# Tiles of the split products moved to one address modulo 512 bytes, and half-height products padded with zero rows, in a two-layer RWKV / Conformer trunk

## The chip, the cores and the metric

One core of a Trainium2 chip runs one program. The metric is the device time of one execution in microseconds (us); a profiled execution shows every instruction of the five engines: TensorE (PE, its weight loads apart as PEld), VectorE (DVE), ScalarE (ACT), GpSimd (POOL) and SyncE (SP), which issues the DMAs. Lower is better.

## The reference, cut to what matters

```
for layer in range(2):                        # x: 512 tokens x 1024 features, float32
    h = rmsnorm(x, g_mix[layer])
    x = x + (rwkv7_time_mix(h) if layer == 0 else conformer_conv(h))
    x = x + memory_cross_attention(rmsnorm(x, g_x[layer]), memn, ...)
    x = x + conv_ffn(rmsnorm(x, g_f[layer]), ...)      # 1024 -> 2 x 2816 -> 1024
return rmsnorm(x, g_final)
# inside the time mix, H = 16 heads of 64 features:
logw  = -softplus(-(w0 + tanh(xw @ w1) @ w2)) - 0.5    # w1: 1024 x 64, w2: 64 x 1024
a     = sigmoid(a0 + (xa @ a1) @ a2)                   # a1: 1024 x 64, a2: 64 x 1024
g     = sigmoid(xg @ g1) @ g2                          # g1: 1024 x 160, g2: 160 x 1024
y     = groupnorm_per_head(recurrence(r, decay, k, v, kk, a))
out   = ((y + sum(r * k * r_k, per head) * v) * g) @ w_o
```

## The kernel before

Features lie on the 128 partitions, the 512 tokens along each partition. The recurrence is computed in chunks of 64 tokens. The order of work is that of the code, with a scheduler's priorities deciding where the streams of two parts meet on an engine.

Every large product is a **split product**. A float32 operand is cast to the type float32r by ACT (its high part) and DVE subtracts the high part from the original (its low part), in `split` (L176, L177); a product is then three float32r matmuls, in `mm3`: high x high (L181), high x low (L182), low x high (L183). The first operand of a matmul is the stationary one (loaded into the array by a weight load of 128 columns, 512 bytes of a partition), the second the moving one (512 columns, 2048 bytes of a partition). In the profile a group is written out<-moving,stationary: `g<-xh,wl` is moving tile xh against weights wl. `wsplit` fetches 512 KB of weights into a `raw` tile and splits it into `wh` and `wl`, two buffers of each. The moving tiles differ by stage: `xh`, `xl` (the normed input of the r, k, v, query, Conformer-in and FFN-in products), `BK` (into w_o), `oh`, `ol` (into the attention's output), `ah`, `al` (into the FFN's second product) and `vh`, `vl` (into the Conformer's second product).

Three small products of the time mix use fewer than 128 rows of the array. In `k_done`, for each of the 8 pairs of heads p, w2 and a2 are each used as a full product with `zw` or `za` (L507: 128 rows, both halves of z, once with the high and once with the low part of w2) and one of 64 rows with `zl` (L508). In `rowbcast` (L475, called twice for each p in `rwkv_out`) a row of 0 and 1 in `selb` spreads a row of per-head numbers over 64 partitions, with 64 rows of the array. In `rwkv_out` the last 32 rows of g2 are a product of 96 rows (L815).

Tiles are placed by pools that stand one behind the other; in a pool the tiles stand one behind the other too, each rounded up to 32 bytes. Where a tile begins follows from all that stand ahead of it. In the built program the operands of the split products begin, modulo 512 bytes, at:

| operands (moving against stationary) | moving | stationary | difference |
|---|---|---|---|
| xh, xl against wh, wl | 32 | 160 | 128 |
| ah, al against wh, wl (FFN, second product) | 160 | 160 | 0 |
| oh, ol against wh, wl (attention output) | 160 | 160 | 0 |
| km against qh, ql (attention scores) | 160 | 160 | 0 |
| vh, vl against wh, wl (Conformer, second product) | 384 | 160 | 288 |
| BK against wh, wl (time mix, w_o) | 256 | 160 | 416 |
| ph, pl against vm (attention values) | 288 | 160 | 384 |

A slice of weights is 512 bytes long and a moving tile 2048, so the difference is the same for all products of a row. Some products are plain float32: `raw` against `kvm` (L931) begins at 160 against 160 in 24 of its products and at 160 against 256 in 8.

Of the kernel before, what the change touches and what calls it, by code (L numbers as in the profile page):

```python
# [8 lines left out]
F32 = mybir.dt.float32  # L9
F32R = mybir.dt.float32r  # L10
# [7 lines left out]
KT = D // 128  # L18
# [8 lines left out]
CW = 31  # L27
KAPPA = float(np.exp(-0.5))
NTMP = 6
# [81 lines left out]
class Builder:  # L111
# [212 lines left out]
    def rwkv(self):  # L324
        nc, a = self.nc, self.a
        with ExitStack() as cx:
            r1 = self.pool(cx, "r1")
# [11 lines left out]
            units = self.key_units(0, mem) + self.value_units(0, mem)  # L339
            for j in range(NU0):  # L340
                units.pop(0)(lambda: t4[:, j % 2, :])
            cpr = self.t(r1, [128, 11 * KT], "cpr")
            hw0, ha0, hka, cka, nkk = (cpr[:, j * KT : (j + 1) * KT] for j in range(5))
            self.cc = (hw0, ha0, hka, cka, nkk)
            vv = lambda n, w=1: self.vecs[:, VEC[n] : VEC[n] + w * KT]
# [8 lines left out]
            h = self.x  # L354
# [5 lines left out]
            rs = self.rstd_tail([acc], 0)  # L360
# [14 lines left out]
            ps = self.ps()  # L375
            for i in range(KT):
                for m, w, o in ((1, w1, 0), (4, a1, 64)):
                    nc.tensor.matmul(ps[o : o + 64, :], w[:, i * 64 : (i + 1) * 64], mix(m, i, "xh", KT),
                                     start=i == 0, stop=i == KT - 1)
# [91 lines left out]

    def rowbcast(self, half, p):
        ps = self.ps("h")
        rows = slice(64 * half, 64 * half + 64)
        self.nc.tensor.matmul(ps, self.selb[rows, p * 128 : (p + 1) * 128], self.rows[rows], start=True, stop=True)  # L475
        return ps

    def k_done(self, p, psk):

        nc, a = self.nc, self.a  # L480
        hw0, ha0, hka, cka, nkk = self.cc
        vv = self.vec
        k, ec = self.AR[:, 0, p, :], self.AR[:, 1, p, :]
        as3 = lambda x_: x_.rearrange("p (c t) -> p c t", t=C)
        nc.scalar.copy(k, psk)
        sq = self.tmp()
        nc.scalar.activation(sq, psk, AF.Square, scale=vv("kk", p))
        pq = self.ps("h")
        for c2 in range(4):
            nc.tensor.matmul(pq[:, 2 * c2 : 2 * c2 + 2], sq[:, c2 * 128 : (c2 + 1) * 128], self.c("head"),  # L490
                             start=True, stop=True)
        rho = self.rho[:, p * NCH : (p + 1) * NCH].rearrange("p (a b) -> p a b", b=2)
        for h in range(2):
            for e in range(2):
                nc.vector.tensor_scalar_max(rho[64 * h : 64 * h + 64, :, e],
                                            pq[64 * e : 64 * e + 64, 0:8].rearrange("p (a b) -> p a b", b=2)[:, :, h], 1e-24)
        nc.vector.reciprocal(self.rho[:, p * NCH : (p + 1) * NCH], self.rho[:, p * NCH : (p + 1) * NCH])
        w2 = self.t(self.r1, [128, 2, 128], "w2", bufs=W2B)
        nc.sync.dma_start(w2, a["wa2"][p])
        ws = self.t(self.gp, [128, 2, 128], "tmp", F32R, bufs=NTMP)  # L500
        nc.scalar.copy(ws, w2)
        pl = []
        for h, z in enumerate((self.zw, self.za)):
            own, oth = slice(64 * h, 64 * h + 64), slice(64 - 64 * h, 128 - 64 * h)
            nc.vector.tensor_tensor(out=ws[oth, h], in0=w2[oth, h], in1=ws[oth, h], op=ALU.subtract)
            ps = self.ps("h")
            nc.tensor.matmul(ps, ws[:, h], z, start=True, stop=False)  # L507
            nc.tensor.matmul(ps, ws[own, h], self.zl[own], start=False, stop=True)  # L508
            pl.append(ps)
        pw, pa = pl  # L510
        th = self.tmp()
        nc.scalar.activation(th, pw, AF.Tanh, bias=hw0[:, p : p + 1], scale=0.5)
        half = self.eps[:, 3:4]
        nc.scalar.activation(th, th, AF.Identity, bias=half, scale=0.5)
        cum = self.tmp()
        nc.vector.tensor_tensor_scan(out=cum, data0=self.c("scan"), data1=th, initial=0.0, op0=ALU.mult, op1=ALU.add)
        nc.scalar.activation(ec, cum, AF.Exp, scale=-KAPPA)
        emc = self.tmp()
        nc.scalar.activation(emc, cum, AF.Exp, scale=KAPPA)
        nc.vector.tensor_copy(self.G[:, p * 8 : p * 8 + 8].unsqueeze(2), as3(ec)[:, :, C - 1 : C])  # L520
        ta = self.tmp()
        nc.scalar.activation(ta, pa, AF.Tanh, bias=ha0[:, p : p + 1], scale=0.5)
        km = self.tmp()
        nc.scalar.activation(km, ta, AF.Identity, bias=cka[:, p : p + 1], scale=hka[:, p : p + 1])
        nc.scalar.activation(ta, ta, AF.Identity, bias=half, scale=0.5)
        BK = self.t(self.r1, [128, NCH, 2, C], "BK", bufs=NP)
        self.bk[p] = BK
        nc.vector.tensor_tensor(out=ta, in0=ta, in1=emc, op=ALU.mult)
        kp = km
        nc.vector.tensor_tensor(out=kp, in0=k, in1=km, op=ALU.mult)  # L530
        for h in range(2):
            rows = slice(64 * h, 64 * h + 64)
            nc.vector.scalar_tensor_tensor(out=BK[rows, :, h, :], in0=as3(k)[rows], scalar=vv("kk", p)[rows],
                                           in1=as3(ta)[rows], op0=ALU.mult, op1=ALU.mult)
            nc.vector.tensor_tensor(out=BK[rows, :, 1 - h, :], in0=as3(kp)[rows], in1=as3(emc)[rows], op=ALU.mult)
        k3, e3 = as3(k), as3(ec)
        nc.vector.scalar_tensor_tensor(out=k3[:, :, 1:], in0=k3[:, :, 1:], scalar=nkk[:, p : p + 1],
                                       in1=e3[:, :, : C - 1], op0=ALU.mult, op1=ALU.mult)
        nc.vector.tensor_scalar_mul(k3[:, :, 0:1], k3[:, :, 0:1], nkk[:, p : p + 1])
# [220 lines left out]
    def rstd_rows(self, tt):  # L760
# [4 lines left out]
        for q in range(2):  # L765
# [6 lines left out]
            for j in range(4):  # L772
                p = q * 4 + j
                nc.tensor.matmul(var[:, 2 * p : 2 * p + 2], sq[:, j, :], self.c("head"), start=True, stop=True)
        rs = self.t(self.gp, [128, 32], "rst", bufs=1)
        nc.vector.memset(rs, 1.0)
        nc.scalar.activation(rs[:, 0:16], var[:, 0:16], AF.Sqrt, bias=self.eps[:, 1:2], scale=1.0 / HD)
        nc.vector.reciprocal(rs[:, 0:16], rs[:, 0:16])
# [7 lines left out]
    def rwkv_out(self):  # L786
        nc, a = self.nc, self.a
        AR, V = self.AR, self.V
        slot = lambda dt=F32: self.t(self.r1, [128, 1024], "c4", dt, bufs=4)
        late, selb = slot(), slot(F32R)  # L790
        nc.sync.dma_start(late, a["late"][:, 0:1024])
        self.selb = selb
        nc.scalar.copy(selb, late)
        g1, g2 = self.gates
        zg1 = self.xtile()
        self.split(g1, *zg1)
        zg2 = self.t(self.gp, [128, T], "xh", F32R, bufs=KT)
        nc.scalar.copy(zg2[0:96], g2[0:96])
        nc.vector.tensor_tensor(out=zg2[32:64], in0=g2[32:64], in1=zg2[32:64], op=ALU.subtract)
        self.filler(FP)  # L800
        outs = []
        for p in range(NP):
# [9 lines left out]
                nc.vector.tensor_tensor(out=lo, in0=raw[64:96, :, 128:256], in1=lo, op=ALU.subtract)  # L812
            pgt = self.ps()
            self.mm3(pgt, gh[:, p % 2, 0:128], gl[:, p % 2, :], *zg1, True, False)
            nc.tensor.matmul(pgt, gh[0:96, p % 2, 128:256], zg2[0:96], start=False, stop=True)  # L815
            pr = self.rowbcast(1, p)
            yn = self.tmp()
            nc.vector.tensor_tensor(out=yn, in0=y, in1=pr, op=ALU.mult)
# [121 lines left out]
    def xattn(self, layer):  # L940
        nc, a = self.nc, self.a
        kd, vd = self.kvd[0, layer], self.kvd[1, layer]
        with ExitStack() as cx:
# [22 lines left out]
            def soft(h):  # L966
                P[h] = self.t(xp, [128, 4, MEM], "P", bufs=2)
                for t2 in range(2):
                    sc = self.ps("h")
                    st = self.t(xp, [128, 8], "st", bufs=4)  # L970
                    for tl in range(2):
                        ts = slice((2 * t2 + tl) * 128, (2 * t2 + tl + 1) * 128)
                        for j in range(2):
# [128 lines left out]
    def conv(self):  # L1102
        nc, a = self.nc, self.a
        PADW = CW - 1
        with ExitStack() as cx:
            up = self.pool(cx, "up")
            y = self.t(up, [128, KT, T], "y")
            cdw = self.t(up, [128, KT * CW], "cdw")
            nc.sync.dma_start(cdw, a["cdw"])
            i2 = self.t(up, [128, 64], "i2")  # L1110
            nc.sync.dma_start(i2, a["i2"])
# [263 lines left out]
```

## Time and profile before

| | |
|---|---|
| median of 3 runs (lowest to highest) | 1730.85 us (1727.83 to 1731.16) |
| the profiled execution: its own time | 1731.13 us |
| its span, first to last instruction | 1729.4 us |
| mean granted TensorE clock | 0.988 of 2.4 GHz |
| busy: PE / weight loads / DVE / ACT / POOL | 1701.2 / 1332.5 / 1097.4 / 773.7 / 68.2 us |
| matmuls (a float32 product counts each pass) | 9662 |
| DMA | 159.77 MB, mean 92 GB/s |

A matmul's duration in the profile holds the time in which the next one is already under way, so two matmuls that follow each other closely overlap. What one costs in a stream is the distance from its start to the next one's start; over a long stretch it is the stretch's length divided by the number of matmuls in it (a window counts those that reach into it, so some 0.4 us belong to the length).

### The profile page before, as it was taken

To read this page: it belongs to the slowest core of one execution; us is meant where nothing else is said; L and a number is where in the kernel's file an instruction comes from. 1 tells how busy PE (TensorE), PEld (TensorE's weight loads), DVE (VectorE), ACT (ScalarE), POOL (GpSimd) and SP (SyncE) were. 2 spreads that over 40 slices of the span, in tenths; PEclk is the share of its full clock that TensorE was granted. 3 is DMA by queue.
4 is the path that set the end of the run, shared out by engine and by line. 5 is a ranking of instruction groups with operands and counts; after the bars stand their busy time and mean duration, and the time that the engine had idled before them with its cause. 6 is when DMAs were issued, how large, how long until landed. Compare 5 with 4: busy or idle time off the path is not lost. (4 is left out here: it accounts for less than half of the span.)

```text
span 1729.4 us, 23930 instructions
## 1 busy us (share of the span) xinstructions
PE 1701.2 (98%) x9662; PEld 1332.5 (77%) x9662; DVE 1097.4 (63%) x1777; ACT 773.7 (45%) x1199; POOL 68.2 (4%) x90
## 2 busy tenths in 40 slices
PE   7999999999999999999999999999999999999998
PEld 5575668887688888888888877767888888888887
DVE  5779885344666567777753358996666677777333
ACT  6765534444434334344332246665444443443222
POOL 0000000000000000000000013440000000000000
PEclk9999998998999999999999999999999999999999
DMA  6323312001523133323323331223422233233332
GB/s 227 120 83 116 100 51 74 26 14 45 158 92 122 51 124 97 91 92 98 98 88 99 93 128 61 61 86 96 136 62 73 88 97 98 88 96 94 91 99 83
DMA packets 55151, 159.77 MB, mean 92 GB/s; under 512 B 6144, under 2 KB 10368, under 8 KB 55040
## 3 DMA queue, kind: packets, MB, share of 16 engines
q1 hardware_dynamic: 55040, 158.24, 29.4%
q8 instruction: 76, 1.25, 0.3%
q14 instruction: 35, 0.29, 0.1%
HBM read 150.55 MB, written 7.67 MB: 91 GB/s over the span
## 5 line engine op out<-in xcount | busy, mean ns | idle before, releaser
L176 ACT CAST wh<-raw 128x1024 fp32r<-128x1024 f32 (+1 forms) x225 | 233.0, 1036 | 533.8 <-PE g L182 426.0
L182 PE MATMUL g<-xl,wh 128*128 128x512 f32 x1152 | 459.0, 398 | 2.9 <-DVE xl L177 2.6
L181 PE MATMUL g<-xh,wh 128*128 128x512 f32 x1152 | 460.4, 401 | 0.4 <-ACT xh L176 0.4
L183 PE MATMUL g<-xh,wl 128*128 128x512 f32 x1152 | 458.7, 398 | 1.6 <-DVE wl L177 1.6
L177 DVE TENSOR_TENSOR wl<-raw,wh 128x1024 fp32r<-128x1024 f32 (+1 forms) x225 | 272.1, 1210 | 173.5 <-ACT wh L176 167.7
L182 PEld LDWEIGHTS g<-xl,wh 128*128 128x128 f32 x1152 | 218.6, 190 | 58.0 <-DVE xl L177 5.1
L183 PEld LDWEIGHTS g<-xh,wl 128*128 128x128 f32 x1152 | 218.5, 190 | 54.0 <-issue 2.2
L181 PEld LDWEIGHTS g<-xh,wh 128*128 128x128 f32 x1152 | 218.7, 190 | 53.6 <-issue 2.0
L181 PE MATMUL g<-ah,wh 128*128 128x512 f32 (+1 forms) x374 | 140.9, 377 | 0.0
L183 PE MATMUL g<-ah,wl 128*128 128x512 f32 (+1 forms) x374 | 140.8, 377 | 0.0
L182 PE MATMUL g<-al,wh 128*128 128x512 f32 (+1 forms) x374 | 140.8, 377 | 0.0
L1045 DVE TENSOR_TENSOR z<-g,rs 128x512 f32<-128x512 f32 x88 | 60.4, 688 | 77.0 <-PE g L183 75.3
L1165 POOL TENSOR_TENSOR dg<-i,wsp 128x256 fp32r<-128x256 f32 x70 | 48.3, 721 | 913.3 <-DVE wsp L1119 828.2
L182 PEld LDWEIGHTS g<-al,wh 128*128 128x128 f32 x374 | 70.4, 188 | 13.0
L183 PEld LDWEIGHTS g<-ah,wl 128*128 128x128 f32 x374 | 70.4, 188 | 12.9
L181 PEld LDWEIGHTS g<-ah,wh 128*128 128x128 f32 x374 | 70.4, 188 | 12.9
L1187 DVE SCALAR_TENSOR_TENSOR h<-u,cdw,h 128x512 f32<-128x512 f32 x98 | 73.8, 753 | 2.3
L176 ACT CAST ah<-tmp 128x512 fp32r<-128x512 f32 x44 | 27.3, 621 | 100.9 <-DVE z L1044 95.8
L321 DVE TENSOR_TENSOR x<-x,g 128x512 f32<-128x512 f32 x39 | 26.8, 688 | 68.7 <-PE g L183 68.6
L1050 DVE SCALAR_TENSOR_TENSOR tmp<-z,fdw,tmp 128x512 f32<-128x512 f32 x88 | 66.0, 752 | 2.9
L1049 DVE SCALAR_TENSOR_TENSOR tmp<-z,fdw,tmp 128x512 f32<-128x512 f32 x88 | 65.5, 746 | 0.4 <-ACT tmp L1048 0.4
L1048 ACT ACTIVATE tmp<-z,fdw 128x512 f32<-128x512 f32 x88 | 63.4, 723 | 2.2 <-DVE z L1045 2.2
(327 smaller groups left out, 2457.3 us busy)
## 6 DMA issues: line engine op xcount, KB each, us to landing
raw<-wi SPq DMA_DIRECT2D x84, 512.0 KB, 3.5
raw<-wo SPq DMA_DIRECT2D x33, 512.0 KB, 3.5
raw<-wv SPq DMA_DIRECT2D x16, 512.0 KB, 3.7
raw<-cwi SPq DMA_DIRECT2D x14, 512.0 KB, 3.5
raw<-wq SPq DMA_DIRECT2D x12, 512.0 KB, 4.5
raw<-wxo SPq DMA_DIRECT2D x12, 512.0 KB, 3.5
raw<-wo SPq DMA_DIRECT2D x16, 384.0 KB, 3.2
raw<-wk SPq DMA_DIRECT2D x10, 512.0 KB, 3.6
```

What stands on the lines that cost most here:

```text
L176: self.nc.scalar.copy(h, src)
L177: self.nc.vector.tensor_tensor(out=l, in0=src, in1=h, op=ALU.subtract)
L181: mm(out, lh, rh, start=start, stop=False)
L182: mm(out, lh, rl, start=False, stop=False)
L183: mm(out, ll, rh, start=False, stop=stop)
L321: self.nc.vector.tensor_tensor(out=self.x[:, n, :], in0=self.x[:, n, :], in1=ps, op=ALU.add)
L1045: nc.vector.tensor_tensor(out=z[:, 2:], in0=ps, in1=rs(), op=ALU.mult)
L1048: nc.scalar.activation(y, z[:, 2:], AF.Copy, scale=cw(2))
L1049: nc.vector.scalar_tensor_tensor(out=y, in0=z[:, 1 : T + 1], scalar=cw(1), in1=y, op0=ALU.mult, op1=ALU.add)
L1050: nc.vector.scalar_tensor_tensor(out=y, in0=z[:, 0:T], scalar=cw(0), in1=y, op0=ALU.mult, op1=ALU.add)
L1165: nc.gpsimd.tensor_tensor(out=dg[:, h], in0=i2.unsqueeze(1).unsqueeze(1).to_broadcast([128, 2, 2, 64]), in1=wsp[:, :, i, h, 2 * g : 2 * g ...
L1187: nc.vector.scalar_tensor_tensor(out=ac, in0=u[:, jt : jt + T], scalar=cw(jt), in1=ac if n else ln["c"], op0=ALU.mult, op1=ALU.add if n el ...
```

## The change

Four small tiles are made larger, so that the tiles behind them begin elsewhere: `cpr` from 352 to 768 bytes, `rst` from 128 to 512, `st` from 32 to 128 (4 buffers), `cdw` from 992 to 1280. Only the first part of each is used, as before. In the built program all operands of the table above then begin at 32 modulo 512, so that every difference is 0. The Conformer's convolution by diagonal matrices (`dg`, L1170) keeps the differences that it had. Of the plain float32 products several get other differences; `raw` against `kvm` goes to 288 in 24 of its products and stays at 96 in 8.

The three small products become products of 128 rows. `ws` gets two more blocks that POOL sets to zero and ACT fills in one half; `selb` becomes two tiles of 1024 columns, each zero in one half, by a POOL memset and an ACT cast of 64 partitions each in place of one cast of 128; `zg2` gets 32 zero rows (the matching rows of g2 are zero already).

```diff
-            cpr = self.t(r1, [128, 11 * KT], "cpr")
+            cpr = self.t(r1, [128, 192], "cpr")[:, : 11 * KT]
...
     def rowbcast(self, half, p):
-        rows = slice(64 * half, 64 * half + 64)
-        self.nc.tensor.matmul(ps, self.selb[rows, p * 128 : (p + 1) * 128], self.rows[rows], start=True, stop=True)
+        self.nc.tensor.matmul(ps, self.selb[half][:, p * 128 : (p + 1) * 128], self.rows, start=True, stop=True)
...
-        ws = self.t(self.gp, [128, 2, 128], "tmp", F32R, bufs=NTMP)
-        nc.scalar.copy(ws, w2)
+        ws = self.t(self.gp, [128, 4, 128], "tmp", F32R, bufs=NTMP)
+        nc.gpsimd.memset(ws[:, 2:4].bitcast(F32), 0.0)
+        nc.scalar.copy(ws[:, 0:2], w2)
...
+            nc.scalar.copy(ws[own, 2 + h], w2[own, h])
...
-            nc.tensor.matmul(ps, ws[own, h], self.zl[own], start=False, stop=True)
+            nc.tensor.matmul(ps, ws[:, 2 + h], self.zl, start=False, stop=True)
...
-        rs = self.t(self.gp, [128, 32], "rst", bufs=1)
+        rs = self.t(self.gp, [128, 128], "rst", bufs=1)[:, 0:32]
...
-        late, selb = slot(), slot(F32R)
+        late = slot()
-        self.selb = selb
-        nc.scalar.copy(selb, late)
+        self.selb = [slot(F32R) for _ in range(2)]
+        for h in range(2):
+            own, oth = slice(64 * h, 64 * h + 64), slice(64 - 64 * h, 128 - 64 * h)
+            nc.gpsimd.memset(self.selb[h][oth].bitcast(F32), 0.0)
+            nc.scalar.copy(self.selb[h][own], late[own])
...
+        nc.gpsimd.memset(zg2[96:128].bitcast(F32), 0.0)
...
-            nc.tensor.matmul(pgt, gh[0:96, p % 2, 128:256], zg2[0:96], start=False, stop=True)
+            nc.tensor.matmul(pgt, gh[:, p % 2, 128:256], zg2, start=False, stop=True)
...
-                    st = self.t(xp, [128, 8], "st", bufs=4)
+                    st = self.t(xp, [128, 32], "st", bufs=4)
...
-            cdw = self.t(up, [128, KT * CW], "cdw")
+            cdw = self.t(up, [128, 320], "cdw")[:, : KT * CW]
```

The instructions of DVE and SP are the same in the same order. On ACT 17 casts are added (16 in `k_done`, one in `rwkv_out`), on POOL 11 memsets. ACT in `k_done` for the second pair of heads, before (`tmp_602` is `ws`, `w_143` the w2 tile):

```order
L487 ACTIVATE tmp_588<-g_490,vecs_59 128x512
L525 ACTIVATE tmp_573<-tmp_573,eps_61 128x512
L501 CAST tmp_602<-w_143_600 128x256
L176 CAST wh_1021<-raw_1019 128x1024
L485 COPY AR_81<-g_652 128x512
L512 ACTIVATE tmp_612<-h_605,cpr_202 128x512
```

and the same place of the change (`tmp_605` is `ws`):

```order
L486 ACTIVATE tmp_591<-g_490,vecs_59 128x512
L526 ACTIVATE tmp_576<-tmp_576,eps_61 128x512
L501 CAST tmp_605<-w_143_603 128x256
L505 CAST tmp_605<-w_143_603 64x128 x2
L484 COPY AR_81<-g_658 128x512
L176 CAST wh_1033<-raw_1031 128x1024
L513 ACTIVATE tmp_618<-h_610,cpr_202 128x512
```

Two casts of 64x128 have come in behind the cast of w2, and here the copy of k has passed the weights' cast. ACT in the seventh of the eight chunks of the recurrence, before (`c_684` is `selb`):

```order
L715 COPY xl_3660<-h_3884 64x256
L668 COPY xh_3991<-AR_81 64x4x64
L793 CAST c_684_4156<-c_683_4155 128x1024
L748 COPY AR_81<-h_3909 128x4x64
L668 COPY xh_3994<-AR_81 64x4x64
L703 COPY tmp_3936<-h_3927 128x256
L715 COPY xl_3661<-h_3938 64x256
```

and of the change (`c_684` and `c_685` are the two tiles of `selb`):

```order
L716 COPY xl_3684<-h_3908 64x256
L669 COPY xh_4015<-AR_81 64x4x64
L797 CAST c_684_4181<-c_683_4179 64x1024
L749 COPY AR_81<-h_3933 128x4x64
L669 COPY xh_4018<-AR_81 64x4x64
L704 COPY tmp_3960<-h_3951 128x256
L797 CAST c_685_4182<-c_683_4179 64x1024
L716 COPY xl_3685<-h_3962 64x256
```

The one cast has become two, the second of which stands three places later, between the copies of X (L704) and of U (L716) of the recurrence.

## Rows read from the trace of the kernel before

**Rows 1.** The page: busy time by engine, and the last chain by line.

```profile
PE 1701.2 (98%) x9662; PEld 1332.5 (77%) x9662; DVE 1097.4 (63%) x1777; ACT 773.7 (45%) x1199; POOL 68.2 (4%) x90
...
PE g L182 11%; PE g L181 11%; PE g L183 11%; PE h L1170 3%; PE kv L931 1%; PE h L181 0%; PE h L183 0%; PE h L182 0%; POOL dg L1165 0%; PE h L239 0%; PE h L248 0%; PE h L995 0%; ACT s L1159 0%; ACT s L1158 0%; DVE x L1273 0%
```

**Rows 2.** By stretch: length; PE, PEld, DVE, ACT, POOL busy (count); clock; DMA share.

```profile
75.00:190.00 115.00, 114.56 (x671) 78.11 (x669) 96.12 (x220) 69.52 (x114) 1.90 (x2) 1.00 0.32 98
440.00:472.00 32.00, 31.23 (x122) 20.27 (x120) 24.54 (x41) 14.13 (x22) 0.00 (x0) 1.00 0.57 177
...
600.00:635.00 35.00, 35.00 (x156) 28.95 (x155) 22.01 (x32) 14.23 (x21) 0.00 (x0) 1.00 0.29 91
700.00:860.00 160.00, 160.00 (x690) 129.73 (x689) 115.32 (x174) 65.43 (x87) 0.00 (x0) 1.00 0.31 96
905.00:1000.00 95.00, 95.00 (x421) 78.67 (x420) 29.14 (x31) 21.68 (x25) 0.00 (x0) 1.00 0.34 98
1010.00:1150.00 140.00, 137.27 (x568) 104.55 (x567) 118.28 (x168) 86.32 (x127) 54.11 (x70) 1.00 0.24 78
```

**Rows 3.** Groups of PE by shape: count, busy us, mean ns, idle before.

```profile
L181 PE MATMUL g<-xh,wh 128*128 128x512 f32 x1152 | 460.4, 401 | 0.4 <-ACT xh L176 0.4
...
L181 PE MATMUL g<-ah,wh 128*128 128x512 f32 x330 | 128.4, 389 | 0.0
...
L181 PE MATMUL g<-oh,wh 128*128 128x512 f32 x128 | 50.0, 391 | 0.0
...
L181 PE MATMUL g<-BK,wh 128*128 128x512 f32 x64 | 27.0, 421 | 1.7 <-DVE tmp L827 1.7
...
L181 PE MATMUL g<-vh,wh 128*128 128x512 f32 x64 | 25.5, 402 | 0.0
```

**Rows 4.** PE in order of time, Conformer's second product: start, duration, instruction.

```profile
1192.06 0.40 PE L181 MATMUL g<-vh,wh 128*128 128x512 f32 x1
...
1193.46 0.40 PE L181 MATMUL g<-vh,wh 128*128 128x512 f32 x1
```

**Rows 5.** PE in order of time, plain float32 products, two stretches.

```profile
1011.98 4.03 PE L931 MATMUL kv<-raw,kvm 128*128 128x512 f32 x9
...
1151.54 5.74 PE L931 MATMUL kv<-raw,kvm 128*128 128x512 f32 x13
```

**Rows 6.** PE in order of time around the second pair's w2 products.

```profile
91.68 0.40 PE L507 MATMUL h<-zw,tmp 128*128 128x512 f32 x1
92.00 0.49 PE L508 MATMUL h<-zl,tmp 64*128 64x512 f32 x1
92.42 0.49 PE L507 MATMUL h<-za,tmp 128*128 128x512 f32 x1
...
93.61 0.39 PE L181 MATMUL g<-xh,wh 128*128 128x512 f32 x1
```

**Rows 7.** PE in order of time around a row broadcast.

```profile
457.30 0.50 PE L475 MATMUL h<-zw,c 64*128 64x512 f32 x1
457.73 0.48 PE L907 MATMUL kv<-wh,raw 128*128 128x256 f32 x1
```

**Rows 8.** PE in order of time, attention output, right behind other products.

```profile
599.64 0.40 PE L183 MATMUL g<-oh,wl 128*128 128x512 f32 x1
...
601.72 0.39 PE L183 MATMUL g<-oh,wl 128*128 128x512 f32 x1
```

**Rows 9.** PE's waits from 75 to 475 us: total, times, longest.

```profile
PE g L181 <- DVE tmp L827: 1.7, 1, 1.7
```

**Rows 10.** Single lines: durations in ns min/median/max, first and last start.

```profile
L501 ACT CAST tmp<-w x8: 391/395/404, 75.7 to 181.9; 128x256 fp32r<-128x256 f32 x8
...
L793 ACT CAST c<-c x1: 1040/1040/1040, 420.0 to 420.0; 128x1024 fp32r<-128x1024 f32 x1
...
L614 POOL MEMSET tt<- x4: 947/950/952, 96.1 to 191.3; 32x1024 f32 x4
```

## The prediction

> **What bounds the kernel now.** I read the page first. TensorE is busy 98% of the span, and the chain that ended last runs over the three lines of the split product in equal shares, 11% each [rows 1]. A busy share near 100% says little where matmuls overlap, so I went on to what one product costs: the number of matmuls in a stretch that holds one kind alone. The reader is to compare three stretches in [rows 2]. In the first FFN product (700 to 860 us, xh against wh and wl) 690 matmuls reach into 160 us: (160 + 0.4) / 690 = 232.5 ns each. In the second (905 to 1000 us, ah) it is 95.4 / 421 = 226.6 ns. The shape is the same, PE is busy without a break in both, and the clock granted is 1.00, the level of 2.4 GHz, in both. Two things differ: the load of the other engines, and where the operands begin. DVE is busy 115.3 of 160 us in the slow stretch and 29.1 of 95 in the fast one. The attention output (600 to 635 us, oh) tells them apart: DVE is busy 22.0 of 35 us there and ACT 14.2 (63% and 41%, against 72% and 41% in the slow stretch), and a product costs 35.4 / 156 = 226.9 ns. The Conformer's second product (vh) is slow: six products from 1192.06 to 1193.46 us are 233 ns each [rows 4]. By the table of addresses, the two fast kinds have moving and stationary operand at the same address modulo 512, and the slow ones do not: differences of 128 and 288. I take this for the cause. So PE sets the time in the long stages, and 2.5% of each product there hang on the address.
>
> The exceptions: in the time mix from 440 to 472 us DVE is busy 24.5 of 32 us, and PE once waits 1.7 us for its product with the gate (L827) [rows 2, 9]; from 75 to 190 us DVE is at 96.1 of 115 us, and from 1010 to 1150 us at 118.3 of 140 [rows 2].
>
> **The change part by part.** *Addresses.* Every split product comes to a difference of 0. The saving of a long stream is 232.5 - 226.7 = 5.8 ns a matmul. The count of xh products is 3 x 1152 = 3456 [rows 3]; by the code 2 x 44 x 8 x 3 = 2112 of them are the FFNs', 384 the queries', 384 the Conformer's first product and 576 the time mix's. FFN: 2112 x 5.8 = 12.2 us, all on PE and all taken.
>
> The other 1344 stand in short runs, cut by other products. Behind a cut the low spacing does not come at once: nine products of oh from 599.64 to 601.72 us take 231 ns each although their difference is 0 [rows 8]. A run of 24 would then save on 15. For queries and Conformer that is 768 x 5.8 x 15/24 = 2.8 us; for the time mix, more cut up and with DVE close, I take half the rate, 576 x 5.8 x 0.31 = 1.0 us. Bounds for the 1344: 0 and 7.8 us.
>
> vh and BK are 3 x 64 products each [rows 3]. vh stands at 233 ns [rows 4]; for BK, slow by its difference as well, I take the same: 384 x 6.5 = 2.5 us.
>
> The plain float32 products change their differences too. `raw` against `kvm` has a difference of 96 at 1012 us and of 0 at 1152 us, and a pass costs (4.03 - 0.59) / 8 = 0.43 us and (5.74 - 0.59) / 12 = 0.43 us [rows 5] (0.59 being taken off for the last one's tail). So I take 0 for them; their bounds are not known better than within 1 us of either sign over the recurrence.
>
> Here the Trainium skill speaks against the change. Its page "SBUF — State Buffer", section "Who interferes with whom", says that PE never waits on another engine at the memory, and "TensorE: Matmul & The Clock Gate", Part 2, that the weight load and the moving operand have independent read ports, so that loading the next weights takes nothing from the running product. By that rule no address would matter and this part would be worth 0. The trace has a difference that goes with the address and not with the load, so I take the trace; the rule is a rival below.
>
> *Padding.* A 64-row product among 128-row ones costs about double. From 91.68 to 93.61 us five products (L507, L508, L507, L508 and the next L183) take 1.93 us [rows 6]; at 232 ns they would take 1.16. That is 0.77 us for each of 8 pairs of heads, 6.2 us. ACT and DVE are the neighbours here and other pairs lie among float32 products, so I take 4.0, with bounds of 0 and 6.2. A row broadcast takes 0.43 us [rows 7] and, like L508, makes the product ahead of it 0.32 instead of 0.23 us [rows 6]: 0.29 us for each of 16, 4.6 us. But there DVE is the one that PE waits for [rows 9], so I take 1.0, with bounds of 0 and 4.6.
>
> By the Trainium skill's page on TensorE ("TensorE: Matmul & The Clock Gate"), section "LDWEIGHTS (loading the stationary operand)", the number of rows doesn't change the time of a load; then padding would be worth 0. The rows show 0.43 against 0.23 us.
>
> *What is added.* Sixteen casts of 64x128 on ACT: nearest is the one of 128x256 at 0.395 us [rows 10], which none of them should exceed, so at most 6.3 us. They lie in 75 to 190 us, where ACT is busy 69.5 of 115 us [rows 2]: nothing on the path, and 6.3 us if that cover were gone. Behind them wait the copy of k and the next weights' cast; wl waits for that, and PE for wl, but two buffers of weights stand ahead. Eight memsets of 128x256 on POOL: the known one, of four times the columns, takes 0.95 us [rows 10], and POOL is busy 1.9 of 115 us [rows 2]. They wait for a free `tmp` slot as the cast of w2 does, which runs 0.39 us ahead of the casts that need them: 0. The cast of `selb` was 1.04 us; two of 1024 columns are 2.1 [rows 10]. The second stands in the recurrence ahead of the copy of U; if it finds no idle time there, the chunk is 1.0 us later, and if it waits for the two memsets as well, 3. I take 0.5. The memset of `zg2` is off any path.
>
> **Sum.** 12.2 + 2.8 + 1.0 + 2.5 + 4.0 + 1.0 - 0.5 = 23.0 us off the profiled execution's 1731.1: 1708.1 us. That execution lies 0.3 us above the median, so the median is forecast at 1708 us, 1.3% less. With every bound at its best: 12.2 + 7.8 + 2.5 + 6.2 + 4.6 = 33.3, 1697 us. With the short runs and the padding worth nothing: 12.2 + 2.5 - 3 = 11.7, 1719 us.
>
> **The rivals.**
>
> *Only the long streams gain.* PE gets faster, but in the time mix and the Conformer DVE, at 84% in both [rows 2], hands over its tiles no sooner, and PE waits instead. For it: the wait at L827 [rows 9]. Against it: PE's idle time there is small, 114.6 busy of 115 us and 137.3 of 140 [rows 2]. Time: 12.2 + 2.5 us and the queries' 1.4, less 0.5: 1715, and up to 1722 with the added work on the path.
>
> *The address does nothing.* The gap between 232.5 and 226.7 ns belongs to the stages for another cause. Then only the padding is left: 5.0 - 0.5 = 4.5 us, 1726 (1720 to 1731). For it: nothing in the rows shows one product at two addresses. Against it: four stages sort by address where they don't sort by load. It is what the page on SBUF, cited above from the Trainium skill, would have.
>
> *It is the place and not the difference* (the other side). Fast were the kinds whose moving operand begins at 160; slow those at 32 and 384. The change moves all to 32. If 32 itself is the slow place, the fast kinds lose 5.8 ns: ah 3 x 330 and its 132 half-size ones, oh 3 x 128 [rows 3], some 1440 products, 8.4 us, and the others gain nothing. With the padding's 5 that is 1735. With the 0.5 of added work it is slower than before as soon as the padding gives less than 8.9 us, and by over 0.2% when it gives less than 5.4; with no padding gain, 1740. Against it: 32 and 160 differ by 128 bytes alone, and there is no reason for 160 to be special other than that the weights stood there.
>
> **How the numbers follow.** The forecast (1697 to 1714) has 0.68, the gain in the long streams alone (1714 to 1722) 0.20, no effect of the address 0.06, the place 0.06. What a measurement of this kernel can tell from no change is about 0.2%, 3.5 us. Faster by more than that are the first two and two thirds of the third: 0.92. The other third, and a third of the fourth, are the same: 0.04. The rest of the fourth is slower: 0.04. The range 1698 to 1720 leaves out the last two cases and the ends of the first two, some 0.18.
>
> **What would show it.** Right: in the first FFN product PE matmuls start 227 ns apart, about 706 in 160 us, and the second one's spacing stays at 227; the attention output and the scores stay as they are; L508 and L475 are 128 rows high, and no matmul beside them starts 0.42 us after another; the 160 us of the FFN stage lose 4 us with DVE's busy time unchanged. Wrong: a spacing of 232 with a difference of 0 (second rival), or of 232 in the stretch of ah as well (third); waits of PE for DVE in the time mix that eat the padding's gain (first); an ACT wait for POOL around the casts of `selb`. I would be wrong by a lot if a cut stream stayed slow far beyond nine products, or if the float32 products of the recurrence felt their new addresses.

## The result, and the profile after

| | before | the change |
|---|---|---|
| median (lowest to highest, executions) | 1730.64 us (1727.83 to 1731.16, 4) | 1710.81 us (1704.39 to 1713.99, 4) |
| ratio to before, 95% interval | | 0.9884 [0.9852, 0.9916] |
| profiled execution: own time, span | 1731.13 us, 1729.4 us | 1704.39 us, 1702.6 us |
| mean granted clock of the executions | .986 to .994 in later runs | .990, .987, .985, .983 |

The change is faster by 1.2%. The profiled execution is the fastest of the four, and its clock is the highest, so its trace shows more than the median has: 26.7 us of span against 19.8 us of median.

The page of the changed kernel, busy time by engine and the last chain by line (to be read against [rows 1]):

```profile
PE 1668.6 (98%) x9662; PEld 1328.1 (78%) x9662; DVE 1096.9 (64%) x1777; ACT 782.5 (46%) x1216; POOL 73.2 (4%) x101
...
PE g L182 11%; PE g L181 11%; PE g L183 11%; PE h L1175 3%; PE kv L936 1%; PE h L181 0%; PE h L183 0%; PE h L182 0%; POOL dg L1170 0%; PE h L239 0%; PE h L248 0%; PE h L1000 0%; ACT s L1164 0%; ACT s L1163 0%; DVE x L1278 0%
```

PE is busy 32.6 us less with the same 9662 matmuls, DVE's work is the same, ACT has its 17 casts more. The span is only 26.7 us shorter, so PE also sits idle 5.9 us more than before. The chain has not moved to another engine.

The windows of the changed kernel, laid over the same work as [rows 2] (columns as there):

```profile
75.00:190.00 115.00, 112.58 (x679) 79.26 (x677) 97.52 (x221) 76.20 (x133) 5.44 (x11) 1.00 0.34 102
440.00:466.00 26.00, 23.94 (x103) 18.51 (x101) 23.54 (x39) 13.18 (x19) 0.00 (x0) 1.00 0.60 189
590.00:625.00 35.00, 35.00 (x156) 29.01 (x155) 22.90 (x33) 14.52 (x21) 0.00 (x0) 1.00 0.28 90
680.00:840.00 160.00, 160.00 (x708) 132.52 (x707) 117.81 (x176) 66.99 (x88) 0.00 (x0) 1.00 0.31 96
885.00:980.00 95.00, 95.00 (x420) 78.69 (x420) 29.42 (x31) 22.17 (x26) 0.00 (x0) 1.00 0.32 97
```

The first FFN product now has 708 matmuls in 160 us: 160.4 / 708 = 226.6 ns, where it was 232.5. The second one (420 in 95 us) and the attention output (156 in 35 us) are as they were. DVE does 117.8 us of work in the 160 us, more than before, and the spacing is at the low value all the same: the load of DVE was not what made the difference.

The groups of PE by shape (against [rows 3]):

```profile
L181 PE MATMUL g<-xh,wh 128*128 128x512 f32 x1152 | 454.0, 395 | 0.6 <-ACT xh L176 0.6
...
L181 PE MATMUL g<-ah,wh 128*128 128x512 f32 x330 | 128.4, 389 | 0.0
...
L181 PE MATMUL g<-vh,wh 128*128 128x512 f32 x64 | 25.1, 395 | 0.0
...
L181 PE MATMUL g<-BK,wh 128*128 128x512 f32 x64 | 25.0, 390 | 2.1 <-DVE tmp L832 2.1
```

xh, vh and BK are shorter; ah is the same to the nanosecond. PE's wait for DVE at the gate (L832, L827 before) has grown from 1.7 us [rows 9] to 2.1, and its wait for the low part of the inputs, first before and then after, from 2.6 to 3.6:

```profile
L182 PE MATMUL g<-xl,wh 128*128 128x512 f32 x1152 | 459.0, 398 | 2.9 <-DVE xl L177 2.6 <-DVE xd L1177 0.3
```

```profile
L182 PE MATMUL g<-xl,wh 128*128 128x512 f32 x1152 | 452.2, 393 | 4.2 <-DVE xl L177 3.6 <-DVE xd L1182 0.5
```

With all the smaller ones, PE's waits for DVE have grown by 3.8 us over the trace, from 14.4 to 18.2.

PE in order of time, around the second pair's w2 products and around a row broadcast (against [rows 6, 7]):

```profile
92.01 0.39 PE L508 MATMUL h<-zw,tmp 128*128 128x512 f32 x1
92.24 0.39 PE L509 MATMUL h<-zl,tmp 128*128 128x512 f32 x1
92.47 0.39 PE L508 MATMUL h<-za,tmp 128*128 128x512 f32 x1
92.70 0.40 PE L509 MATMUL h<-zl,tmp 128*128 128x512 f32 x1
92.93 0.39 PE L181 MATMUL g<-xh,wh 128*128 128x512 f32 x1
...
451.70 0.39 PE L474 MATMUL h<-zw,c 128*128 128x512 f32 x1
451.93 2.32 PE L912 MATMUL kv<-wh,raw 128*128 128x256 f32 x10
```

With 128 rows each of them takes 0.23 us, and neither they nor the products beside them stand 0.42 us behind a neighbour any more.

**Where the 26.7 us come from.** I compared the start of the same instruction in both traces, stage by stage. First to last w2 product: 113.99 us before, 110.74 after. First broadcast to first BK: 28.99, 26.56. First BK to last: 48.27, 43.61, of which 3.4 us are half of a stretch of 6.8 us at 1.2 GHz from 473 us, which the trace of the change does not have (the window of 470 to 482 us in before, below, has a clock of 0.72). From the last oh to the first ah, which is an FFN's first product: 247.44, 241.41, and in the second layer 247.45, 241.41. Attention with its queries: 0.92 and 0.94 us less, the Conformer's first product 0.86, vh 1.23. The w2 products begin 1.1 us later than before, and the recurrence (from the last w2 product to the first broadcast) is 1.4 us shorter.

```profile
470.00:482.00 12.00, 10.27 (x29) 7.00 (x28) 8.67 (x13) 4.31 (x6) 0.00 (x0) 0.72 0.60 209
```

### The profile page after: what moved, and what is told of

It is laid out like the page before. It is cut to its first block, busy times and chain, and to the rows that moved or that the text cites. A ratio compares the mean times of both kernels' runs of the same rounds, so it can differ in the third digit from the quotient of the medians.

```text
span 1702.6 us, 23980 instructions
## 1 busy us (share of the span) xinstructions
PE 1668.6 (98%) x9662; PEld 1328.1 (78%) x9662; DVE 1096.9 (64%) x1777; ACT 782.5 (46%) x1216; POOL 73.2 (4%) x101
## 5 line engine op out<-in xcount | busy, mean ns | idle before, releaser
L182 PE MATMUL g<-xl,wh 128*128 128x512 f32 x1152 | 452.2, 393 | 4.2 <-DVE xl L177 3.6
L181 PE MATMUL g<-xh,wh 128*128 128x512 f32 x1152 | 454.0, 395 | 0.6 <-ACT xh L176 0.6
L183 PE MATMUL g<-xh,wl 128*128 128x512 f32 x1152 | 451.9, 392 | 1.6 <-DVE wl L177 1.6
L182 PEld LDWEIGHTS g<-xl,wh 128*128 128x128 f32 x1152 | 217.5, 189 | 54.0 <-DVE xl L177 6.6
L183 PEld LDWEIGHTS g<-xh,wl 128*128 128x128 f32 x1152 | 217.5, 189 | 49.3 <-DVE wl L177 2.3
L181 PEld LDWEIGHTS g<-xh,wh 128*128 128x128 f32 x1152 | 217.4, 189 | 48.8 <-ACT xh L176 1.7
L181 PE MATMUL g<-ah,wh 128*128 128x512 f32 (+1 forms) x374 | 140.9, 377 | 0.0
L182 PE MATMUL g<-al,wh 128*128 128x512 f32 (+1 forms) x374 | 140.8, 377 | 0.0
L183 PE MATMUL g<-ah,wl 128*128 128x512 f32 (+1 forms) x374 | 140.8, 377 | 0.0
L182 PEld LDWEIGHTS g<-al,wh 128*128 128x128 f32 x374 | 70.4, 188 | 13.0
L183 PEld LDWEIGHTS g<-ah,wl 128*128 128x128 f32 x374 | 70.4, 188 | 12.9
L181 PEld LDWEIGHTS g<-ah,wh 128*128 128x128 f32 x374 | 70.4, 188 | 12.7
L1170 POOL TENSOR_TENSOR dg<-i,wsp 128x256 fp32r<-128x256 f32 x70 | 48.3, 723 | 668.2 <-DVE wsp L1124 584.1
```

The lines of the kernel that those rows point to most:

```text
L181: mm(out, lh, rh, start=start, stop=False)
L182: mm(out, lh, rl, start=False, stop=False)
L183: mm(out, ll, rh, start=False, stop=stop)
L1170: nc.gpsimd.tensor_tensor(out=dg[:, h], in0=i2.unsqueeze(1).unsqueeze(1).to_broadcast([128, 2, 2, 64]), in1=wsp[:, :, i, h, 2 * g : 2 * g ...
```

## The experiments

Medians are given with the kernel before timed on the same chip. The clock is the mean granted clock of an execution.

### The two halves of the change apart

*Addresses alone:* the four tiles of the change, and none of its padding, added to the kernel before.

```diff
-            cpr = self.t(r1, [128, 11 * KT], "cpr")
+            cpr = self.t(r1, [128, 192], "cpr")[:, : 11 * KT]
...
-        rs = self.t(self.gp, [128, 32], "rst", bufs=1)
+        rs = self.t(self.gp, [128, 128], "rst", bufs=1)[:, 0:32]
...
-                    st = self.t(xp, [128, 8], "st", bufs=4)
+                    st = self.t(xp, [128, 32], "st", bufs=4)
...
-            cdw = self.t(up, [128, KT * CW], "cdw")
+            cdw = self.t(up, [128, 320], "cdw")[:, : KT * CW]
```

> The addresses of the change with the small products left at 64 and 96 rows as before. If the difference modulo 512 is what the split products pay for: 227 ns a product in all long streams, both FFNs 12 us shorter together as in the change, about 1714 to 1716 us in all, 15 to 17 below before (12.1 FFNs, 1.2 w_o, 1.2 vh, 1 to 2 in the queries and the Conformer). If the padding carries more than its 4 to 6 us (the rival: it also keeps the granted clock up in the time mix), this kernel stays at 1720 or above.

*Padding alone:* the change with those four lines taken back.

> The padding of the change with the addresses of before. If padding and addresses add up: 232 ns a product of xh as before, FFNs as before, 1724 to 1727 us (4 to 7 below before, all of it ahead of the attention). If the padding's gain is eaten in the time mix by VectorE, within 2 us of before (1729 to 1731).

| | median | before | ratio, 95% interval |
|---|---|---|---|
| addresses alone | 1714.93 us | 1726.96 us | 0.9913 [0.9887, 0.9939] |
| padding alone | 1720.83 us | 1726.96 us | 0.9958 [0.9943, 0.9972] |

The FFN's first product, addresses alone (first row) and padding alone (second fence):

```profile
690.00:850.00 160.00, 160.00 (x707) 132.54 (x706) 117.70 (x178) 66.67 (x87) 0.00 (x0) 1.00 0.31 99
```

```profile
690.00:850.00 160.00, 160.00 (x690) 129.73 (x689) 115.45 (x174) 64.74 (x87) 0.00 (x0) 1.00 0.31 96
```

Four larger tiles, whose added parts no instruction uses, bring 707 matmuls into the stretch; the padding leaves the 690 of before. So the address is the cause of the spacing. The addresses gave 12.0 us of median, less than the 15 to 17 expected; the time expected (1714 to 1716 us) came only because before took 1727 us here and not 1731. The padding's whole gain lies in the time mix: from the last oh on, its trace runs 8.6 us ahead of before to the end. Of these, 2.8 us are in the stage of w2 and 2.6 in that of the broadcast; another 2.0 lie in the stage of BK, some 1.7 of them less time at 1.2 GHz, and 1.2 in the recurrence. The padding gave 6.1 us of median, more than the two terms of 5.0 that I had for it, and its 1720.83 us are below the range expected (1724 to 1727), again beside a faster before.

### The two paddings apart

The addresses with the padding of w2 alone, and with that of the broadcast and the gate alone.

```diff
-            nc.tensor.matmul(ps, ws[own, h], self.zl[own], start=False, stop=True)
+            nc.tensor.matmul(ps, ws[:, 2 + h], self.zl, start=False, stop=True)
```

> The change with the row broadcast and the gate's last rows left as before (one tile of 0 and 1, 64 and 96 rows); addresses and padded w2 products are kept. If the broadcast's padding is worth about 1 us because VectorE sets the pace there: 1 us above the change. If PE sets it: 4 to 5 us above the change.

```diff
-        self.nc.tensor.matmul(ps, self.selb[rows, p * 128 : (p + 1) * 128], self.rows[rows], start=True, stop=True)
+        self.nc.tensor.matmul(ps, self.selb[half][:, p * 128 : (p + 1) * 128], self.rows, start=True, stop=True)
```

> The change with the w2 products left at 64 rows; addresses and padded broadcast are kept. If the w2 padding is worth 3 to 4 us of PE time: 3 to 4 us above the change, lost between 75 and 195 us. If ACT and VectorE hide it: within 1 us of the change.

With w2 alone: 1713.22 us, 0.9922 [0.9905, 0.9939]. With the broadcast and the gate alone: 1711.09 us, 0.9905 [0.9885, 0.9925]. The medians scatter with the clock, so the stages tell more. First to last w2 product is 0.35 us shorter than before without the padding and 3.25 with it: it is worth 2.9 us, where 3 to 4 were expected. First broadcast to first BK is 29.0 us in the two kernels without that padding and 26.4 to 26.7 in those with it: 2.4 us, between the 1 and the 4 to 5 expected.

### Which difference of addresses

The change with other sizes of the four tiles, and small tiles ahead of the attention's and the FFN's, so that every stage has a difference of its own.

```diff
+            shim = self.t(xp, [128, (480, 352)[layer] // 4], "shim")
+            nc.vector.memset(shim[:, 0:1], 0.0)
...
+            shim = self.t(ap, [128, (448, 288)[layer] // 4], "shim")
+            nc.vector.memset(shim[:, 0:1], 0.0)
```

> The change with other tile sizes, so that each stage has a difference (stationary less moving, modulo 512) of its own: xh 192, oh of layer 0 32, ah of layer 0 64, vh 96, oh of layer 1 160, ah of layer 1 224. If only equality is fast: every stage at 230 to 235 ns a product, ah for the first time too. If nearness counts: 32 and 64 near 227 and the far ones at 232 or more. If the place of the moving tile counts and not the difference: ah of layer 0, whose moving tile begins at 160 as before, stays at 227.

The second has 192, 32 and 160, 384 bytes there.

> As the run before with other differences: xh 256, oh of layer 0 320, ah of layer 0 352, vh 448, oh of layer 1 480, ah of layer 1 128 (its moving tile at 160 again). If only equality is fast: every stage at 230 to 235 ns, and ah of layer 1 at the 232 that xh had with a difference of 128. If half of 512 is as good as none, xh is at 227. If one of them falls below 227, there is a better distance than none.

FFN first product, FFN second product and attention output of the first of these kernels (differences 192, 64, 32):

```profile
690.00:850.00 160.00, 160.00 (x700) 131.27 (x700) 117.14 (x177) 66.78 (x87) 0.00 (x0) 1.00 0.33 97
895.00:990.00 95.00, 95.00 (x409) 76.55 (x408) 29.14 (x31) 20.84 (x25) 0.00 (x0) 1.00 0.31 94
595.00:630.00 35.00, 35.00 (x152) 28.20 (x151) 23.10 (x34) 14.35 (x21) 0.00 (x0) 1.00 0.30 96
```

and FFN first and second product of the second (differences 256, 352):

```profile
690.00:850.00 160.00, 160.00 (x707) 132.51 (x706) 117.08 (x177) 67.74 (x89) 0.00 (x0) 1.00 0.32 99
895.00:990.00 95.00, 95.00 (x407) 76.35 (x407) 28.18 (x30) 20.87 (x24) 0.00 (x0) 1.00 0.31 97
```

As in the prediction, length plus 0.4 us over count: 229.1 ns at 192, 233.3 at 64, 232.9 at 32; 226.9 at 256, 234.4 at 352. With the other stages, counted from start to start:

| difference, bytes | ns from start to start |
|---|---|
| 0, 256 | 227 |
| 192, 448 | 229 |
| 32, 64, 96, 128, 160, 224, 288, 320, 352, 384, 416, 480 | 232 to 235 |

So 256 does as well as 0, and 448 as 192: what counts is the difference modulo 256, not 512, and the table of the change asks for more than it needs. ah is slow here with its moving tile at 160, where it was fast before: the place is not the cause. No difference is faster than 0. This is read from long streams; a matched address does not help everywhere. The attention's 96 products with vm, 384 in before and 0 in the change, stand among others in runs of 4 on the mean, and take 232.5 ns in before and 231.9 in the change, so nothing of their address's gain came. The two kernels took 1720.42 and 1721.04 us in one execution each, beside 1728.29 of before.

### The high or the low weights

A tile of 128 bytes ahead of `wl` in the change: xh and xl against wh stay at 0, xh against wl goes to 128.

```diff
+            if not hasattr(self, "wshim"):
+                self.wshim = self.t(self.wp, [128, 32], "wshim", bufs=1)
+                nc.vector.memset(self.wshim[:, 0:1], 0.0)
```

> The change with 128 bytes between wh and wl, and the tiles behind them. xh has a difference of 0 to wh and 128 to wl; ah, oh, vh and BK have 384 to wh and 0 to wl. If a product pays for the weight load that runs under it (the next product's weights against its own moving tile): in the stage of xh the start of L182 to the start of L183 is the long one (about 240) and the other two are near 227; in the stage of ah it is the other way round, two long and L182 to L183 short. If it pays for its own weights: in the stage of xh L183 to the next L181 is the long one. If both hang on the whole pattern: all three long in both.

PE in order of time in the FFN's first product:

```profile
699.76 0.39 PE L181 MATMUL g<-xh,wh 128*128 128x512 f32 x1
699.99 0.40 PE L182 MATMUL g<-xl,wh 128*128 128x512 f32 x1
700.22 0.40 PE L183 MATMUL g<-xh,wl 128*128 128x512 f32 x1
...
701.84 0.39 PE L181 MATMUL g<-xh,wh 128*128 128x512 f32 x1
```

Nine products take 2.08 us, 231 ns each. Over the stage the step from L181 to L182 is 227.2 ns, from L182 to L183 232.5 and from L183 to L181 234.0. One product in three has the difference, two steps in three are long; none of the three patterns expected for this stage came. In the second product, where wh has the difference (384) and wl has none, all three steps are long, 232 to 235. In both stages a step is long as soon as one of its two products is mismatched; whether the cost arises through a product's own operands or through the load that runs beneath it, these two patterns don't separate. The kernel took 1728.52 us in one execution, as much as before (1728.29), although it has the padding: ah and oh, fast in before, have become slow (first to last ah of layer 0 is 122.95 us against 119.50).

### The change once more, and where some of its gain goes

The change's executions differ by 0.6%, and with their clock, so I timed it again beside a version with the recurrence's float32 tiles back at the addresses they had before.

> The change itself, beside the next kernel on one chip. By its profile it should stand some 23 us below before at an equal mean granted clock; its median was 20 below, at clocks of 0.983 to 0.990 against 0.987 to 0.994 for before. If that lower clock belongs to the change, its runs again lie at 0.983 to 0.991 with a median 18 to 21 below before; if it was chance, at 0.987 to 0.994 and 23 to 24 below.

```diff
+            shim = self.t(r1, [128, 32], "shim")
+            nc.vector.memset(shim[:, 0:1], 0.0)
...
-            cpr = self.t(r1, [128, 192], "cpr")[:, : 11 * KT]
+            cpr = self.t(r1, [128, 11 * KT], "cpr")
```

> The change with 128 bytes ahead of the time mix's own tiles and cpr at its old size, so that the plain float32 products of the recurrence have the differences of before (BK against wh then 288 instead of 0, 1.2 us more). If the float32 addresses cost clock in the recurrence: clocks as before, 0.987 to 0.994, and a median 2 to 4 us below the change. If they cost nothing: clocks as the change's, and a median 1 us above it.

| | median | clocks | ratio, 95% interval |
|---|---|---|---|
| before | 1726.70 us | mean .990 | |
| the change | 1710.25 us (1699.37 to 1714.46) | .983 to .993, mean .986 | 0.9893 [0.9867, 0.9920] |
| with the old float32 addresses | 1712.58 us | .982 to .986, mean .984 | 0.9912 [0.9898, 0.9926] |

The change's execution at .993 took 1699.37 us, that at .983 1714.46. The clock is lower than before's on the mean, and the float32 addresses of the recurrence are not why.

The next kernel makes the r, k and v products of the time mix slow again and leaves the split products behind them fast, but for BK (differences 416 and 160): the weights of the time mix are read 128 bytes further in, from tiles 256 bytes wider.

```diff
+    woff = 32
+
+    def wt(self, tag):
+        return self.t(self.wp, [128, 1088], tag, F32R, bufs=2)[:, self.woff : self.woff + 1024]
...
-            h = self.t(self.wp, [128, 1024], "wh", F32R, bufs=2)
-            l = self.t(self.wp, [128, 1024], "wl", F32R, bufs=2)
+            h = self.wt("wh")
+            l = self.wt("wl")
...
+            self.woff = 0
```

> The change, but the time mix reads its r, k, v and w_o weights 128 bytes further in wider tiles: there the operands of the split products differ by 128 or 384 (BK by 416 or 160), which the runs so far show as slow (232 to 234 ns). Everything behind the time mix differs by 0 or 256 and should cost 227 ns a product. Theory 1 (the shorter products of the time mix are what loses the clock there): the mean granted clock goes back to .987 to .994 and the median to 1704 to 1708 us, since 2 to 4.5 us are lost in the products and 4 to 5 us of half clock are gone. Theory 2 (the clock is lost for another cause, the start addresses or chance): the clock stays at .983 to .988 and the median is 1712 to 1715 us. Both: FFN first products at 227 ns with differences of 0 and 256.

It took 1705.10 us (clocks .987 to .992), 0.9878 [0.9860, 0.9897]: the median is below the change's, with 576 products slower, but the two intervals overlap. As other tiles have moved too, the last two kernels differ in one number, `woff`: 32 (128 bytes) and 64 (256 bytes). Their instructions stand in the same order on every engine, and the addresses of these 576 products alone differ.

```diff
-    woff = 32
+    woff = 64
```

> The kernel f3_mix_slow once more, beside f5_mix_fast, which differs from it in one number: where the weights of the time mix's r, k and v products are read. Differences there 128 and 384: the products cost 232 to 234 ns. Theory 1 (faster products in the time mix lose the clock there): clock .987 to .992, median 1703 to 1708 us. Theory 2 (the clocks of f3_mix_slow came from its other tiles and start times, or by chance): the clock is that of f5_mix_fast within .001.

> f3_mix_slow with the weights of the time mix's r, k and v products 256 bytes further in instead of 128: differences of 256, so 227 to 229 ns a product, with every tile and every instruction's place the same. Theory 1: clock .983 to .988 and a median of 1708 to 1713 us, although its r, k, v products need some 3 us less. Theory 2: clock as in f4_mix_slow_again and a median 1 to 3.3 us below it.

| time mix's products | median | clocks | ratio, 95% interval |
|---|---|---|---|
| slow (difference 128, 384; 232.5 ns) | 1705.35 us (1703.38 to 1710.99) | .987 to .992 | 0.9877 [0.9857, 0.9898] |
| fast (difference 0, 256; 228.6 ns) | 1713.14 us (1710.35 to 1715.08) | .982 to .985 | 0.9918 [0.9901, 0.9936] |

The windows of the kernel with the slow products (the last column but two is the granted clock):

```profile
200.00:260.00 60.00, 56.40 (x551) 37.34 (x548) 42.16 (x81) 18.34 (x29) 0.00 (x0) 0.90 0.15 46
300.00:308.00 8.00, 8.00 (x52) 6.30 (x51) 0.00 (x0) 1.22 (x3) 0.00 (x0) 0.65 0.01 2
310.00:345.00 35.00, 34.45 (x550) 29.21 (x549) 15.24 (x30) 17.27 (x39) 0.00 (x0) 1.00 0.05 17
345.00:356.00 11.00, 11.00 (x144) 8.12 (x143) 3.06 (x9) 5.21 (x13) 0.00 (x0) 1.00 0.18 49
...
410.00:425.00 15.00, 14.81 (x247) 12.22 (x246) 8.15 (x18) 10.46 (x23) 0.52 (x1) 1.00 0.01 2
```

and of the one with the fast products:

```profile
200.00:260.00 60.00, 55.94 (x529) 37.16 (x529) 42.18 (x81) 18.33 (x29) 0.00 (x0) 0.89 0.14 46
300.00:308.00 8.00, 8.00 (x46) 6.22 (x47) 0.00 (x0) 1.08 (x2) 0.00 (x0) 0.50 0.01 2
310.00:345.00 35.00, 34.45 (x546) 29.08 (x544) 14.82 (x29) 16.85 (x37) 0.00 (x0) 1.00 0.08 30
345.00:356.00 11.00, 11.00 (x52) 7.17 (x54) 0.94 (x4) 4.21 (x10) 0.00 (x0) 0.54 0.14 41
...
410.00:425.00 15.00, 15.00 (x146) 11.31 (x143) 4.18 (x11) 5.27 (x12) 0.80 (x1) 0.66 0.00 1
```

Until the end of r's products they go nearly alike: from the first product of k to the last of r the fast one needs 184.3 us against 185.0, so the faster products give 0.6 us there. In 300 to 308 us, among the last of v's products, the fast one is longer at the level of 1.2 GHz (0.50 against 0.65). Behind 314 us the products are the same in both, and there the fast one has two stretches with much of it that are at 2.4 GHz throughout in the slow one: 11 us with 52 matmuls against 144, and 15 us with 146 against 247. What PE did in the 35 us ahead of the first of them reads alike, 34.45 us busy in both. The two traces part in the recurrence alone: from the last w2 product to the first broadcast it takes 251.69 us in the slow one and 262.66 in the fast one, and every stage behind it agrees within 0.3 us. The first theory's numbers came (the fast one's median 0.1 us above its range), the second's (equal clocks) did not: with operands at a matched address, the r, k, v products of the time mix cost 7.8 us of median, and the two intervals don't overlap.

The address does not settle a single execution. The change's own two traces differ in the same stage, 251.36 us at a mean clock of .990 and 257.46 at .986. What the address moves is how often which clock comes. With these products at differences of 0 or 256 (seven kernels, 40 executions) 34 executions have a mean clock of .987 or less; with 128 or 384 (before, the padding alone and the slow kernel above, 70 executions with a clock on record) 64 have .988 or more. Why the clock falls behind the faster products, these rows don't show.

## Why the prediction was right, point by point

**The bound and the cause.** PE's spacing in long streams hung on the address, as read from four stages of the trace of before; the addresses alone and the padding alone confirm it. The rivals that the address does nothing (1726 us) and that the place decides (1735 us) are out, by the 707 against 690 and by ah slow at 160. The rule of the Trainium skill's page "SBUF — State Buffer", section "Who interferes with whom", as the prediction read it, would have had the addresses alone at no gain; they gave 12.0 us, so the measurement decides against that reading for these products. The extra time of a 64-row product went with its padding too (0.43 and 0.23 us), and it was not in the weight load, whose records take 183 ns for 64 rows and 188 for 128. One thing in the first part was wrong: the period. It is 256, which the four stages of before could not tell, as 288, 128, 384 and 416 are all mismatched by either.

**The terms:**

| term | predicted | shown by the stages |
|---|---|---|
| FFN addresses | 12.2 | 12.1 |
| queries, attention, Conformer first product | 2.8 | 2.7 |
| vh and BK | 2.5 | 1.2 + 1.3 |
| padding of w2 | 4.0 | 2.9 |
| padding of the broadcast | 1.0 | 2.4 |
| time mix's xh products | 1.0 | 0.6, and then time lost to the clock (below) |
| added casts and memsets | -0.5 | nothing seen |

The BK entry is 192 products by 6.8 ns (233.5 against 226.7). All but the clock add up to 23.2 us; the prediction's sum was 23.0. That the sums are so close is partly luck: errors of 1.1 and 0.4 us too much stand against 1.4 and 0.5 too little. The median shows less, 19.8 us here and 16.5 when it was timed again.

**The step that failed** is the time mix: "for the time mix, more cut up and with DVE close, I take half the rate". The rate was of the right size (0.6 us) and the stretch behind it was left out. I had set a change of the granted clock in the recurrence nowhere in the sum, though the trace of before falls to 1.2 GHz there as well (0.86 in 250 to 310 us, 0.94 in 350 to 440):

```profile
250.00:310.00 60.00, 56.93 (x427) 45.27 (x426) 30.43 (x54) 24.95 (x35) 0.00 (x0) 0.86 0.23 72
...
350.00:440.00 90.00, 89.19 (x1389) 72.85 (x1386) 38.95 (x83) 41.12 (x96) 0.00 (x0) 0.94 0.10 29
```

So the median is 2.8 us above the forecast. What the clock takes is measured in two places: 7.8 us of median between the last two kernels, and 6.1 us of the recurrence between the change's own two traces. The change's medians (mean 1710.5 us) also stand 5.3 us above 1705.2 with the mix's products slow, which have 1.3 us of BK to make up besides; but as those intervals overlap, that difference alone would not show it.

**Mis-sized terms.** The broadcast: the prediction let DVE set the pace there because of one wait of PE for it. PE was busy 31.2 of 32 us [rows 2], and that was the better sign: it set the pace for all but the wait. After the padding PE is busy 23.9 of 26 us, so only now is DVE near. The w2 padding: the 32 steps from a w2 product to the next one fell from 14.06 to 10.04 us, the 4.0 forecast, but the padding makes the stage as a whole only 2.9 us shorter. The rest went into waits: with the padding alone PE sits idle 1.6 us in this stage, in short waits for ACT and DVE, where it was 0.4 before.

**The first rival**, that only the long streams gain (1715 us), forecast a time that the change comes near (1710.8), for a cause that is there only in part. It takes some 7 us of the sum away; PE's waits for DVE grew by 3.8 us, and the terms that the rival takes away (the padding, the time mix, half of the queries and the Conformer) still came, as the table shows.

## What to carry to other kernels

Where PE is the bound, divide a long window by its count of matmuls, stage by stage; a step of a few nanoseconds between like stages is worth a look at where their operands begin, and the size of a small tile ahead of them can be all that the repair takes. Products of 64 rows among those of 128 are worth filling up with zero rows, if PE sets the pace there. And a faster stage can hand time back in a later one: compare the granted clock of several executions, not of one trace, before a gain is added up. Here the kernel with the slow products ahead of the recurrence took 7.8 us less than its twin with fast ones, and the lowest medians of all, 1705.1 and 1705.4 us, are its own (the change's interval overlaps theirs).

## What was not expected of the hardware

In long streams, a float32r product of 512 columns started 227 ns behind the one before it where stationary and moving operand began at the same address modulo 256 bytes, 229 ns at 192, and 232 to 235 at twelve other differences. One mismatched product in three made two steps of three long (232.5 and 234.0 ns). A product of 64 rows among 128-row ones took 0.43 us, with 128 rows 0.23. And 4 ns less for each of 576 products was followed, some 30 and 100 us after the last of them and in other work, by stretches of 11 and 15 us with a granted clock of 0.54 and 0.66, where the otherwise equal kernel had 1.00; what links the two stays open.
